# A hybrid decoder layer on one core: the convolutions of token blocks 1 to 3 move into the MLP blocks

## The chip, the cores and the metric

The kernel runs on one core of a Trainium2 chip. The metric is device time in microseconds (us) for one execution of the whole layer; the time before is 3008.22 us, the median of three runs (3004.48 to 3009.67). A core has a matmul engine (PE, with its weight loads shown as PEld), three engines for elementwise work (DVE, ACT, POOL) and SP, whose queue issues the DMAs. Each engine works through its own queue in order.

## The reference

One layer on x of 2048 tokens by 1024 channels, in float32. After an RMSNorm with scale and shift, one projection feeds three mixers, whose outputs are concatenated, projected by W_out and added to x; then a gated MLP and a last RMSNorm. The mixer that matters here is C:

```
a, b = split(u);  h = a * sigmoid(b)                       # 256 channels
h = causal depthwise conv of h over tokens, width 31, + cv_b
h = (h - mean) * rsqrt(var + EPS) * ln_w + ln_b            # over the 256 channels
o_c = h * sigmoid(h)
x = x + g1 * (concat[o_a, o_b, o_c] @ W_out)
h = rmsnorm(x) * (1 + sc2) + sh2
x = x + g2 * (relu(h @ W1)^2 @ W2)
```

Mixer A is a gated linear recurrence (HGRN) with four heads; mixer B is attention over the 256 keys of each query that an indexer scores highest.

## The kernel before

The 2048 tokens are four blocks of 512. First the four input blocks run one after the other, each a series of projection units (24 matmuls of 128x512 for a unit of 128 output channels), whose results are evicted by ACT and DVE. Behind the units run generators in named queues: the HGRN heads ("fast"), the convolution ("conv"), the modulation of later stages ("ada"), and index scores, top-k search and attention of the query tiles ("idx", "tk", "at"). After each unit `step()` gives each queue a credit in ns (`rates`), and a generator runs on until its yields have used the credit up. Then come the out block 0 and four MLP blocks. An MLP block has eight groups g, each with four first-layer units (24 matmuls) and one second-layer part (96 matmuls); towards its end `prep` loads the mixer outputs of the next token block and the out block of that block runs between groups 6 and 7. Index scores, top-k and attention of the later tiles go on behind MLP blocks 0 to 2.

The order in each engine's queue is not the order of the program: a scheduler lays the instructions out by a modelled timeline, with priorities. So any edit moves instructions far from it too.

Projections use each operand as a high and a low part (`hi`, `lo`), three products. Weights are split the first time they are used (ACT casts `whi`, L316; POOL subtracts `wlo`, L317) and the parts are stored in DRAM and reloaded as `wk` later; for the MLP weights the first time is MLP block 0. The hidden tiles are split in the same way (`hh` on ACT, `hl` on POOL, L269).

The convolution of a block (`conv_gen`) has two halves of 128 channels. Of its 31 taps, DVE does the even ones into `cacc` (L552, L564); ACT does the odd ones into `ctap` (L561, or L558 for the first, into `cside`) and POOL adds them into `cside` (L562). There is one `ctap` buffer, so the next tap on ACT waits for POOL's add. Then follow mean and variance by small matmuls, and the LayerNorm and swish, whose result goes to DRAM (`mx_d`) until the out block reads it. The input is the tile `hc` of 30 halo columns and 512 new ones, made by the eviction `ev_ca` (L543); the last 30 columns go to `halo` for the next block. Before, each block's convolution is queued when its `hc` is made, in its own input block, with a rate of 2002 (`CR`), beside the HGRN heads. An HGRN head is a chain between DVE and PE: each of seven levels scales half of q (L638) and half of k (L639) on DVE and then multiplies them on PE (L673, L681).

The tag `xt` of the pool `xio` has four buffers of 128x1024 floats. They hold x of the next input block during an input block, x of the out block, and at the end of an MLP block the final norm's weight, the gate and the rows of the output.

## Time and profile before

| what | us |
|---|---|
| median of three runs | 3008.22 |
| the profiled execution's own time | 3010.64 |
| its span, first to last instruction | 3008.9 |
| PE busy in it | 2828.1 |
| DVE, ACT, POOL busy | 1621.1, 1250.3, 1148.7 |
| mean granted PE clock (1 is full) | 0.971 |

In the profile a row of a table by stage has a stretch of the span, its length, the busy time of each engine in it with the number of instructions, the granted clock of PE and the share of the DMA engines. A row of a group has the line, the engine, the tiles written and read, the shapes and the count, then the busy time and the mean of one in ns, then the idle time of the engine just before them and what ended it. A row of the waits has the waiting engine, tile and line, what released it, and the sum, number and longest of the waits. A row of a timeline has start and length, and in brackets the idle time before it.

In the span the input blocks end at about 1090 us and the out block 0 runs into the first MLP block; MLP blocks 0 to 3 run from about 1140, 1590, 2100 and 2590 us. The taps of the convolutions of blocks 1, 2 and 3 stand between 389 and 483, 671 and 771, and 927 and 1008 us.

### The profile page before, as it was taken

What the parts mean: (1) busy time and instruction counts of PE and PEld (TensorE: products, weight loads), DVE (VectorE), ACT (ScalarE), POOL (GpSimd) and SP (SyncE); (2) the same over time, 40 slices, a digit from 0 to 9 for tenths busy, and PEclk for the clock granted to TensorE, in tenths of its full rate; (3) what the DMA queues carried; (4) which work ended last, traced back from release to release, by engine and by line L of the source; (5) the groups of instructions that cost most, each with busy time, mean ns of one, the idle gap of its engine ahead of it and who ended that gap; (6) DMA issues with size and microseconds to landing.
All of it is one profiled execution on the core that took longest, in us unless ns stands there. A gap on an engine that the chain in (4) does not pass through costs nothing.

```text
span 3008.9 us, 42529 instructions
## 1 busy us (share of the span) xinstructions
PE 2828.1 (94%) x14200; PEld 2343.3 (78%) x14200; DVE 1621.1 (54%) x3306; ACT 1250.3 (42%) x2586; POOL 1148.7 (38%) x1051
## 2 busy tenths in 40 slices
PE   5988989898899989999998999999999999999998
PEld 4867868686787877788776888877788888788887
DVE  7695487868447343847758646485944211221113
ACT  4445545435322325455536443444553333231112
POOL 7574143216313254566547422223432223311112
PEclk9998989999999999999999999999999999999999
DMA  8866666575654586899978966777786667685565
GB/s 284 266 202 208 216 185 204 184 243 180 207 173 152 171 273 213 267 288 291 292 239 278 304 202 205 228 225 229 239 289 209 224 206 229 220 274 178 188 204 187
DMA packets 424199, 681.25 MB, mean 226 GB/s; under 512 B 43351, under 2 KB 171420, under 8 KB 423964
## 3 DMA queue, kind: packets, MB, share of 16 engines
q1 hardware_dynamic: 423808, 678.33, 69.8%
q8 instruction: 113, 1.85, 0.2%
q14 instruction: 122, 1.00, 0.1%
q10 hardware_dynamic: 156, 0.07, 0.0%
HBM read 525.40 MB, written 152.84 MB: 225 GB/s over the span
## 4 chain that ended last, share of the span: by engine, by line
PE 42%; DVE 3%; DMA 2%; issue 1%; ACT 1%; POOL 1%; SPq 0%; POOLq 0%; DVEq 0%; ACTq 0%
PE mm L1252 13%; PE mm L391 13%; PE ax L1252 7%; PE ax L391 4%; PE po L977 1%; PE at L965 1%; PE at L943 1%; PE at L1252 1%; PE ix L786 1%; DVE s L793 1%; DMA xo<-x_d 1%; DMA wk<-wk_d 1%; DMA wraw<-in_mlp_w_dram 0%; SPq L106 0%; DVE acc L1396 0%
## 5 line engine op out<-in xcount | busy, mean ns | idle before, releaser
L391 PE MATMUL mm<-ah,wk 128*128 128x512 f32 x2256 | 602.2, 401 | 15.0 <-DVE adrow L744 4.5
L391 PEld LDWEIGHTS mm<-ah,wk 128*128 128x128 f32 x2256 | 422.7, 191 | 103.0 <-DVE adrow L744 4.7
L317 POOL TENSOR_TENSOR wlo<-wraw,whi 128x512 fp32r<-128x512 f32 x210 | 290.0, 1400 | 170.3 <-ACT whi L316 106.5
L269 POOL TENSOR_TENSOR hl<-hr,hh 128x512 fp32r<-128x512 f32 x128 | 168.7, 1319 | 445.3 <-ACT hh L261 417.2
L975 POOL TENSOR_TENSOR pT<-L,pT 128x512 fp32r<-128x512 f32 (+3 forms) x160 | 197.1, 1234 | 298.0 <-ACT pT L974 186.8
L391 PE MATMUL mm<-al,wk 128*128 128x512 f32 x1128 | 307.9, 396 | 0.0
L793 DVE SCALAR_TENSOR_TENSOR s<-r,iw_s,s 128x512 f32<-128x512 f32 (+3 forms) x266 | 243.8, 916 | 110.7 <-ACT r L788 102.7
L1252 PE MATMUL mm<-wk,hh 128*128 128x512 f32 x920 | 281.0, 399 | 1.7 <-DMA wk<-wk_d 1.3
L391 PEld LDWEIGHTS mm<-al,wk 128*128 128x128 f32 x1128 | 211.5, 191 | 42.8
L945 DVE CUSTOM_DVE_ANT_0 L<-at,bias 128x512 f32<-128x512 f32 (+3 forms) x152 | 93.7, 620 | 223.5 <-PE at L943 179.9
L562 POOL TENSOR_TENSOR cside<-cside,ctap 128x512 f32<-128x512 f32 x112 | 163.1, 1456 | 109.7 <-ACT ctap L561 96.3
L1252 PEld LDWEIGHTS mm<-wk,hh 128*128 128x128 f32 x920 | 170.7, 189 | 41.1 <-DMA wk<-wk_d 2.3
L788 ACT ACTIVATE r<-ix 128x512 f32<-128x512 f32 (+3 forms) x256 | 133.1, 553 | 158.6 <-PE ix L786 120.2
L1396 DVE TENSOR_TENSOR acc<-acc,ax 128x512 f32<-128x512 f32 x81 | 55.4, 683 | 237.2 <-PE ax L1252 236.4
L1376 ACT ACTIVATE hr<-mm 128x512 f32<-128x512 f32 x96 | 57.2, 596 | 301.7 <-PE mm L391 301.0
L316 ACT CAST whi<-wraw 128x512 fp32r<-128x512 f32 x210 | 121.5, 618 | 134.1 <-DMA wraw<-in_mlp_w_dram 40.3
L1252 PE MATMUL ax<-wk,hh 128*128 128x512 f32 x552 | 175.8, 399 | 0.3 <-DVE acc L1396 0.3
L895 DVE TENSOR_SCALAR_CACHE_REDUCE cum<-s,ssm 128x384 bf16<-128x384 f32 (+13 forms) x112 | 165.4, 1477 | 9.4 <-POOL s L797 7.1
L1396 DVE TENSOR_TENSOR acc<-acc,mm 128x512 f32<-128x512 f32 x135 | 91.0, 684 | 143.2 <-PE mm L1252 142.6
L973 ACT COPY L<-at 128x512 f32<-128x512 f32 (+3 forms) x160 | 82.8, 522 | 160.8 <-PE at L965 159.1
L1252 PE MATMUL mm<-wk,hl 128*128 128x512 f32 x460 | 149.1, 397 | 0.0
L959 ACT ACTIVATE L<-L,nmx 128x512 f32<-128x512 f32 (+3 forms) x160 | 103.8, 650 | 107.0 <-DVE nmx L954 106.6
(359 smaller groups left out, 6017.2 us busy)
## 6 DMA issues: line engine op xcount, KB each, us to landing
wk<-wk_d SPq DMA_DIRECT2D x800, 256.0 KB
wk<-wk_d SPq DMA_DIRECT2D x198, 512.0 KB
wk_d<-whi SPq DMA_DIRECT2D x210, 256.0 KB
wk_d<-wlo SPq DMA_DIRECT2D x210, 256.0 KB
wraw<-in_mlp_w_dram SPq DMA_DIRECT2D x68, 512.0 KB
kc<-sk_d SPq DMA_DIRECT2D x112, 256.0 KB
vc<-v_d SPq DMA_DIRECT2D x112, 256.0 KB
adw<-in_ada_w_dram SPq DMA_DIRECT2D x128, 128.0 KB
```

The costliest lines, as they stand in the source:

```text
L269: e.tensor_tensor(lo[:, i:j], src[:, i:j], hi[:, i:j].bitcast(F32), OP.subtract)
L316: A.copy(hi, src)
L317: G.tensor_tensor(lo, src, hi.bitcast(F32), OP.subtract)
L391: T.matmul(ps, ww[k], aa[k], start=(n == 0 and k0 == 0), stop=(n == len(order) - 1 and k1 == NK))
L562: G.tensor_tensor(side, side, tap, OP.add)
L788: A.activation(r[:, :w], ps[:, :w], AF.Relu, scale=32.0 ** -0.5)
L793: V.scalar_tensor_tensor(s[:, c0:c0 + w], r[:, :w], iw, s[:, c0:c0 + w], op0=OP.mult, op1=OP.add)
L895: V.tensor_scalar(dump, s, t, -AIM - i * STEP, op0=OP.is_ge, op1=OP.add, accum_out=d)
L959: A.activation(lt[:, :w], lt[:, :w], AF.Exp, bias=nmx, accum_out=sm[:, cb:cb + 1])
L975: G.tensor_tensor(pT[:, :nt, 1], lv, pT[:, :nt, 0].bitcast(F32), OP.subtract)
L1252: T.matmul(ps, aa[f][:, tok * P:(tok + 1) * P], ww[i], start=(first and n == 0), stop=(last and n == 5))
L1396: V.tensor_tensor(dst, dst, src, OP.add)
```

## The change

`ev_ca` stores `hc` of blocks 1 to 3 in DRAM (`hc_d`), and the generator is queued there for block 0 alone. When MLP block b begins, the generator for block b + 1 is queued, with a rate of 950 (`CM`); what is left of it is run out at `prep`. A convolution there takes four `xt` tiles: two receive `hc` (and hold the small results later), one the two sums of DVE, one the side sum and the tap. Its three small products go to the `at` banks of PSUM. Block 0's convolution stays where it was, with its old tiles. The arithmetic is the same.

```diff
+    hc_d = [[dram([P, TAPS - 1 + TB], F32, f"hc_d{b}_{m}") for m in range(2)] for b in range(NB)]
...
         V.tensor_tensor(hc[:, TAPS - 1:], ps, conv[m], OP.mult)
-        G.tensor_copy(halo[:, m, :], hc[:, TB:])
+        if b + 1 < NB:
+            G.tensor_copy(halo[:, m, :], hc[:, TB:])
+        if b:
+            dma(hc_d[b][m], hc)
         conv[m] = hc
...
+    def conv_tiles_late(b):
+        wide = [xp.tile([P, 2, TB], F32, tag="xt", bufs=4, name=nm("cl")) for _ in range(4)]
+        flat = [w.rearrange("p a n -> p (a n)") for w in wide]
+        hcs = [w[:, :TAPS - 1 + TB] for w in flat[:2]]
+        for m in range(2):
+            dma(hcs[m], hc_d[b][m])
+        work = wide[3]
+        cus = [flat[0][:, :TB], flat[1][:, :TB], work[:, 1], work[:, 0], flat[0][:, :TB], flat[1][:, :TB]]
+        return (hcs, [wide[2][:, m] for m in range(2)], lambda: work[:, 0], lambda: work[:, 1], lambda: cus.pop(0),
+                lambda: flat[0][:, D - 4:], lambda i: ps_at())
...
     def conv_gen(b):
-        accs = []
+        hcs, accs, new_side, new_tap, new_cu, new_rs, ps_c = (conv_tiles_late if b else conv_tiles)(b)
...
-            if ev is ev_ca and m == 1:
+            if ev is ev_ca and m == 1 and b == 0:
                 queues["conv"].append(conv_gen(b))
...
     for b in range(NB):
+        if b + 1 < NB:
+            queues["conv"].append(conv_gen(b + 1))
+            rates["conv"] = CM
         for ev in mlp_block(b):
             if ev == "prep":
+                drain("conv")
                 prep_out(b + 1)
```

The queue of DVE in input block 3, at the levels of HGRN head 0 (`q`, `k`) beside which `hc` is made. Before:

```order
L639 TENSOR_TENSOR k_9583<-k_9583,fb_9806 128x64x4
L564 SCALAR_TENSOR_TENSOR cacc_10417<-hc_9984,cvc,cacc_10417 128x512
L564 SCALAR_TENSOR_TENSOR cacc_9995<-hc_9928,cvc,cacc_9995 128x512
L564 SCALAR_TENSOR_TENSOR cacc_10417<-hc_9984,cvc,cacc_10417 128x512
L564 SCALAR_TENSOR_TENSOR cacc_9995<-hc_9928,cvc,cacc_9995 128x512
L564 SCALAR_TENSOR_TENSOR cacc_10417<-hc_9984,cvc,cacc_10417 128x512
L564 SCALAR_TENSOR_TENSOR cacc_9995<-hc_9928,cvc,cacc_9995 128x512
L612 TENSOR_SCALAR f_10050<-f_10050 128x512
```

And now, at the same two levels and the next one (L659 and L660 are the old L638 and L639, L696 the old L675, L633 the old L612):

```order
L660 TENSOR_TENSOR k_9273<-k_9273,fb_9496 128x64x4
L544 TENSOR_TENSOR hc_9618<-mm_9584,csg_9512 128x512
L696 COPY_PREDICATED at_9466<-lmask,ax_9567 128x32x8
L659 TENSOR_TENSOR q_9310<-q_9310,fb_9496 128x4x8x8
L660 TENSOR_TENSOR k_9273<-k_9273,fb_9496 128x32x8
L544 TENSOR_TENSOR hc_9674<-mm_9640,csg_9565 128x512
L696 COPY_PREDICATED at_9466<-lmask,ax_9597 128x16x16
```

The taps (L564) between one level's k and the next are gone; the levels stand next to each other.

The queue of POOL at the start of MLP block 0, from the first weight half (`wlo`) on. Before:

```order
L317 TENSOR_TENSOR wlo_11905<-wraw_11838,whi_11904 128x512
L317 TENSOR_TENSOR wlo_11909<-wraw_11838,whi_11908 128x512
L317 TENSOR_TENSOR wlo_11962<-wraw_11902,whi_11961 128x512
L269 TENSOR_TENSOR hl_11874<-hr_11875,hh_11873 128x512
L317 TENSOR_TENSOR wlo_11966<-wraw_11902,whi_11965 128x512
L269 TENSOR_TENSOR hl_11938<-hr_11939,hh_11937 128x512
```

Now (L318 and L270 are the old L317 and L269; L584 is the add into the side sum, in an `xt` tile named `cl`):

```order
L584 TENSOR_TENSOR cl_11417<-cl_11417 128x512
L318 TENSOR_TENSOR wlo_11445<-wraw_11367,whi_11444 128x512
L584 TENSOR_TENSOR cl_11417<-cl_11417 128x512 x2
L318 TENSOR_TENSOR wlo_11449<-wraw_11367,whi_11448 128x512
L584 TENSOR_TENSOR cl_11417<-cl_11417 128x512
L318 TENSOR_TENSOR wlo_11506<-wraw_11442,whi_11505 128x512
L270 TENSOR_TENSOR hl_11403<-hr_11404,hh_11402 128x512
L318 TENSOR_TENSOR wlo_11510<-wraw_11442,whi_11509 128x512
L584 TENSOR_TENSOR cl_11417<-cl_11417 128x512
```

The adds of the convolution of block 1 now stand one or two at a time between the weight halves and the hidden tiles of MLP block 0; between the first and the last of its 28 adds stand 30 of the weight halves and 9 of the `hl`. On DVE the taps of that convolution follow each other in the same place:

```order
L586 SCALAR_TENSOR_TENSOR cl_11416<-cl_11414,cvc,cl_11416 128x512
L586 SCALAR_TENSOR_TENSOR cl_11416<-cl_11415,cvc,cl_11416 128x512
L586 SCALAR_TENSOR_TENSOR cl_11416<-cl_11414,cvc,cl_11416 128x512
L586 SCALAR_TENSOR_TENSOR cl_11416<-cl_11415,cvc,cl_11416 128x512
L812 TENSOR_SCALAR s_11429<-r_11434,iw_s 128x512
L586 SCALAR_TENSOR_TENSOR cl_11416<-cl_11414,cvc,cl_11416 128x512
L586 SCALAR_TENSOR_TENSOR cl_11416<-cl_11415,cvc,cl_11416 128x512
```

L586 is the old L564 and L812 the first row of the indexer's scores; of the rows of this convolution on DVE, 25 taps stand in a run ahead of that L812 with one other row among them.

More of the change, by code (lines that the diff above doesn't have):

```diff
@@ L63 @@
 CT = 2
-CR = 2002
+CR, CM = 2002, 950.0
 LP = 0
@@ L543, in ev_ca, with conv_tiles @@
         V.tensor_tensor(hc[:, TAPS - 1:], ps, conv[m], OP.mult)
-        G.tensor_copy(halo[:, m, :], hc[:, TB:])
+        if b + 1 < NB:
+            G.tensor_copy(halo[:, m, :], hc[:, TB:])
+        if b:
+            dma(hc_d[b][m], hc)
         conv[m] = hc
+    def conv_tiles(b):
+        hcs = [conv[m] for m in range(2)]
+        accs = [hp.tile([P, TB], F32, tag=f"csg{m}", bufs=1, name=nm("cacc")) for m in range(2)]
+        return (hcs, accs, lambda: hp.tile([P, TB], F32, tag="cside", bufs=1, name=nm("cside")),
+                lambda: hp.tile([P, TB], F32, tag="ctap", bufs=CB, name=nm("ctap")), lambda: st("cu", 2),
+                lambda: hp.tile([P, 4], F32, tag="crs", bufs=1, name=nm("crs")), ps_xp)
+    def conv_tiles_late(b):
[8 more added lines that the diff above has]
+                lambda: flat[0][:, D - 4:], lambda i: ps_at())
     def conv_gen(b):
-        accs = []
+        hcs, accs, new_side, new_tap, new_cu, new_rs, ps_c = (conv_tiles_late if b else conv_tiles)(b)
         for m in range(2):
-            hc = conv[m]
-            acc = hp.tile([P, TB], F32, tag=f"csg{m}", bufs=1, name=nm("cacc"))
+            hc = hcs[m]
+            acc = accs[m]
             V.tensor_scalar(acc, hc[:, 0:TB], cvc[:, m, 0:1], col("cvb", m), op0=OP.mult, op1=OP.add)
@@ L556, in conv_gen @@
                     if side is None:
-                        side = hp.tile([P, TB], F32, tag="cside", bufs=1, name=nm("cside"))
+                        side = new_side()
                         A.mul(side, hc[:, w:w + TB], cvc[:, m, w:w + 1])
                     else:
-                        tap = hp.tile([P, TB], F32, tag="ctap", bufs=CB, name=nm("ctap"))
+                        tap = new_tap()
                         A.mul(tap, hc[:, w:w + TB], cvc[:, m, w:w + 1])
@@ L569, in conv_gen @@
                 V.tensor_tensor(acc, acc, side, OP.add)
-            accs.append(acc)
         yield 1200
-        tot = st("cside", 1)
+        tot = new_side()
         G.tensor_tensor(tot, accs[0], accs[1], OP.add)
-        pm = ps_xp(4)
+        pm = ps_c(4)
         T.matmul(pm, o256.to_broadcast([P, P]), tot, start=True, stop=True)
@@ L579, in conv_gen @@
         for m in range(2):
-            sq = st("cu", 2)
+            sq = new_cu()
             A.activation(sq, accs[m], AF.Square)
@@ L584, in conv_gen @@
         yield 1500
-        pv = ps_xp(5)
+        pv = ps_c(5)
         for t in range(4):
             T.matmul(pv[:, t:t + 1], sqs[0][:, t * P:(t + 1) * P], ones[:, 0:1], start=True, stop=True)
-        rc = hp.tile([P, 4], F32, tag="crs", bufs=1, name=nm("crs"))
+        rc = new_rs()
         V.tensor_copy(rc, pv[:, :4])
@@ L591, in conv_gen @@
         yield 1500
-        rs = ps_xp(6)
+        rs = ps_c(6)
         for t in range(4):
```

4 lines of the change are left out of this document (2 added, 2 removed).

## The prediction

> **What bounds the kernel now.** I read the page first, then a table of busy time by stage, then the waits of PE and the timelines where PE stands.
>
> ```profile
> span 3008.9 us, 42529 instructions
> PE 2828.1 (94%) x14200; PEld 2343.3 (78%) x14200; DVE 1621.1 (54%) x3306; ACT 1250.3 (42%) x2586; POOL 1148.7 (38%) x1051
> ...
> 300.00:1140.00 840.00, 765.48 (x4447) 653.29 (x4446) 524.11 (x1155) 345.06 (x766) 282.45 (x283) 0.95 0.61 196
> 1140.00:1590.00 450.00, 437.86 (x2002) 355.65 (x2001) 271.16 (x540) 238.86 (x476) 265.61 (x221) 0.99 0.86 273
> 1590.00:2100.00 510.00, 495.75 (x2328) 404.07 (x2327) 322.99 (x654) 237.59 (x501) 178.41 (x167) 0.98 0.74 236
> 2100.00:2590.00 490.00, 483.70 (x2292) 394.64 (x2291) 193.90 (x395) 195.50 (x407) 162.83 (x156) 0.99 0.71 232
> ```
>
> Columns of the stage rows: length, then busy time of PE, PEld, DVE, ACT, POOL, the granted clock, DMA share and GB/s. PE sets the time nearly everywhere. MLP blocks 0, 1 and 2 (the last three rows, each with the out block behind it) leave it idle for 12, 14 and 6 us at a clock of 0.98 to 0.99; the input blocks 1 to 3 (300 to 1140) leave it idle for 75 us of 840 and at 0.95. So there is something to win in the input blocks, and little slack to lose in the MLP blocks. The change takes work of DVE, ACT and POOL from the first place to the second. No matmul of the main stream is added or removed, so only PE's standing and its clock can change.
>
> **Part 1: what leaves the input blocks.** I cut 300 to 1140 at the first and last convolution tap of blocks 1, 2 and 3: the second, fourth and sixth rows hold a convolution each, the others none.
>
> ```profile
> 300.00:389.00 89.00, 88.32 (x531) 76.38 (x530) 42.02 (x120) 46.45 (x108) 17.64 (x35) 0.99 0.69 223
> 389.00:483.00 94.00, 78.83 (x403) 64.63 (x402) 86.70 (x149) 52.90 (x99) 52.13 (x46) 0.89 0.62 190
> 483.00:671.00 188.00, 170.84 (x1064) 148.00 (x1063) 134.60 (x401) 76.89 (x191) 38.00 (x52) 0.96 0.64 205
> 671.00:771.00 100.00, 83.83 (x443) 68.61 (x441) 81.41 (x147) 56.04 (x107) 59.55 (x48) 0.93 0.54 177
> 771.00:927.00 156.00, 148.69 (x906) 129.87 (x907) 58.89 (x137) 41.84 (x109) 25.11 (x25) 0.96 0.59 193
> 927.00:1008.00 81.00, 74.98 (x418) 64.29 (x417) 61.83 (x91) 33.27 (x62) 41.45 (x33) 0.96 0.50 161
> 1008.00:1140.00 132.00, 119.99 (x694) 101.52 (x694) 58.64 (x113) 37.66 (x91) 48.56 (x46) 0.94 0.62 209
> ```
>
> I measure what PE gave as busy time times clock. With a convolution: 78.83 x 0.89 + 83.83 x 0.93 + 74.98 x 0.96 = 220.1 us of full-speed work in 275 us, so 54.9 us lost, 20%. Without: 506.9 in 565, so 58.1 us lost, 10%. DVE is busy for 84% of the first kind of stretch and 52% of the second. What leaves, per group:
>
> ```profile
> L562 POOL TENSOR_TENSOR cside<-cside,ctap 128x512 f32<-128x512 f32 x84 | 122.3, 1455 | 86.6 <-ACT ctap L561 78.0 <-ACT cside L558 6.5 <-DMA mx_d<-r 1.9
> L564 DVE SCALAR_TENSOR_TENSOR cacc<-hc,cvc,cacc 128x512 f32<-128x512 f32 x90 | 91.0, 1032 | 0.3
> L561 ACT ACTIVATE ctap<-hc,cvc 128x512 f32<-128x512 f32 x84 | 60.7, 723 | 78.1 <-POOL cside L562 77.6
> sum 275.00, DVE 99.95 ACT 0.00 POOL 3.62; mean DVE 33.32 ACT 0.00 POOL 1.21
> ```
>
> The last row is the sum over the three stretches for the tile cacc alone: 100 us of DVE, 33.3 a block. POOL loses 122 us of adds and ACT 61 us of taps, besides 78 us in which ACT, which works in order, stood before the next tap because the one ctap buffer was still being read by POOL. Is it these rows that hold PE? Three waits of the stretches 389 to 483 and 671 to 771, and the timeline of the longest wait in the third:
>
> ```profile
> PE ax L695 <- DVE k L639: 4.6, 1, 4.6
> PE mm L391 <- ACT k L611: 3.6, 1, 3.6
> PE mm L391 <- DVE adrow L744: 4.5, 1, 4.5
> ...
> 942.84 1.49 DVE L639 TENSOR_TENSOR k<-k,fb 128x256 f32<-128x256 f32 x1
> 944.25 6.13 DVE L564 SCALAR_TENSOR_TENSOR cacc<-hc,cvc,cacc 128x512 f32<-128x512 f32 x6
> 951.73 2.44 DVE L564 SCALAR_TENSOR_TENSOR cacc<-hc,cvc,cacc 128x512 f32<-128x512 f32 x2
> 954.43 1.84 DVE L564 SCALAR_TENSOR_TENSOR cacc<-hc,cvc,cacc 128x512 f32<-128x512 f32 x1
> 956.86 0.41 DVE L639 TENSOR_TENSOR k<-k,fb 128x256 f32<-128x256 f32 x1
> 957.42 1.94 PE L673 MATMUL ax<-q,k 128*128 128x64 f32 x8 [4.74 <-DVE k L639]
> ```
>
> Between two L639 steps of one HGRN head (14 us apart) DVE did nine taps, 10.4 us, and PE stood 4.74 us for the second step. The four longest waits, 4.7, 4.6, 4.5 and 3.6, are 17.4 us. In the new order of DVE these taps are gone and the HGRN levels follow each other. The value I take: the 220.1 us of full-speed work in the convolution stretches will run at the 90% of the others, in 220.1 / 0.897 = 245.4 us, a gain of **29.6 us**. Ends: 54.9 if nothing at all is lost there any more; 5 if the HGRN chain, which DVE also carries in the stretches without a tap, takes the waits over. The value is nearest to the rows of the same stage without a convolution.
>
> The stretch at 389 has the four longest waits' worst clock, 0.89. The Trainium skill, "TensorE: Matmul & The Clock Gate", section "What's actually happening", has the clock halved only after an idle window of about 3.4 us. By that rule, as an estimate, only those four waits cost clock too, 1.7 us each, and the gain would be 17.4 + 6.8 = 24 us; the rows give more because many short waits go with them.
>
> **Part 2: what arrives in the MLP blocks.** The same 33 us of DVE, 41 us of POOL adds and 20 us of ACT taps stand in MLP blocks 0, 1 and 2, from the first unit of the block. What a loaded DVE costs PE there I read from rows of 60 us:
>
> ```profile
> 1210.00:1270.00 60.00, 56.09 (x240) 44.80 (x239) 50.29 (x118) 30.62 (x56) 31.92 (x26) 0.97 0.79 253
> 1270.00:1330.00 60.00, 59.98 (x278) 49.18 (x277) 31.57 (x75) 35.59 (x68) 40.44 (x35) 1.00 0.96 314
> 1390.00:1450.00 60.00, 60.00 (x286) 49.47 (x285) 46.20 (x94) 36.37 (x76) 40.75 (x36) 1.00 0.94 302
> 1450.00:1510.00 60.00, 57.04 (x261) 46.16 (x260) 47.08 (x94) 30.67 (x61) 33.10 (x28) 1.00 0.88 276
> 1830.00:1890.00 60.00, 60.00 (x283) 49.07 (x282) 48.14 (x106) 25.90 (x55) 14.08 (x15) 1.00 0.69 212
> 2130.00:2190.00 60.00, 55.60 (x257) 43.20 (x257) 49.02 (x89) 32.47 (x66) 27.14 (x21) 0.94 0.68 218
> 2190.00:2250.00 60.00, 59.41 (x291) 48.77 (x290) 26.64 (x50) 32.81 (x72) 21.67 (x21) 1.00 0.85 282
> ```
>
> With DVE at 46 to 50 us (five rows) PE's full-speed work falls short by 5.6, 0, 3.0, 0 and 7.7 us, mean 3.3; with DVE at 27 to 32 (two rows) by 0 and 0.6. So one such window lifted costs 3 us. The new order lays the DVE taps nearly in one run at the start of the block, so I count one window for each block: 3 us for each of the MLP blocks 1 and 2. Spread out at 14 us a window it would be 2.4 windows, 7 us a block.
>
> MLP block 0 is the tight one, because POOL splits the weights there for the first time:
>
> ```profile
> L317 POOL TENSOR_TENSOR wlo<-wraw,whi 128x512 fp32r<-128x512 f32 x210 | 290.0, 1400 | 170.3 <-ACT whi L316 106.5 <-PE mm L1252 20.8 <-PE ax L1252 16.7
> L269 POOL TENSOR_TENSOR hl<-hr,hh 128x512 fp32r<-128x512 f32 x128 | 168.7, 1319 | 445.3 <-ACT hh L261 417.2 <-DMA wk<-wk_d 26.6 <-PE mm L391 1.0
> 2690.46 5.48 PE mm L391 x24
> ...
> 2734.67 5.48 PE mm L391 x24
> ```
>
> In the new order 30 weight halves and 9 hl stand on POOL between the first and the last of the convolution's 28 adds: 30 x 1.400 + 9 x 1.319 + 28 x 1.455 = 94.6 us. PE's work for those 15 weight pieces is 9 first-layer units of 5.45 us and 6 second-layer pieces of (44.2 - 4 x 5.45) / 4 = 5.6 us (the last two rows are one group of eight units apart, 44.2 us), 82.7 us; the stage gives PE 437.9 us for 8 x 44.2 + 45 = 399 us of main stream (the out block's 192 matmuls at the second layer's rate are 45), so 10% other work lies between: 91 us. POOL has no slack there, 94.6 against 91. I take 8 us for this block: 3 as above, and 5, one unit, for weights that come late. Ends: 0, as in the row at 1390 with POOL at 41 of 60; 41 if all adds delay the splits.
>
> The Trainium skill, "SBUF — State Buffer", section "Who interferes with whom", speaks against the move: a DVE instruction with two SBUF inputs waits out a GpSimd instruction that reads SBUF. The trace agrees as far as the taps go (mean 1032 ns where the last one above took 1.84 us). By it, as an estimate, thirty taps beside a POOL that never rests would each last to about 1.8 us, and the run of DVE grow from 33 to some 55 us, 2.2 windows in place of one, 4 us more.
>
> Smaller parts, together 0: six stores and six loads of 128x542 floats (277 KB, at the stages' 196 to 273 GB/s 1.0 to 1.4 us each, 14 us if all lay bare) lie beside DMA engines at 61% and 86%, and a load stands ahead of weights that are asked for a unit early. The x of the out block now waits on SP for the convolution's result to be stored, about half an MLP block before it is used; if that cover were gone, 4 x 524 KB at 236 GB/s, 9 us a block. Three small matmul groups per convolution move with it, and their work is PE's in either place. Where a result of POOL is late for them, PE stands as it does now.
>
> **Sum**, on the profiled execution's own 3010.64 us (span 3008.9): -29.6 + 8 + 3 + 3 = -15.6, so **2995 us**. The median of the runs shown, 3008.22, lies 2.4 us lower; I name **2994**. What a measurement can tell from no change is about 0.2%, 6 us.
>
> **Rivals.** *No change*: the HGRN chain keeps the waits (the stretch 1008 to 1140 loses 9% without a tap), the gain is 10 to 15, the cost 14: 3007 to 3012. For it: half of PE's loss in the input blocks is in stretches without taps. Against: the 10.4 us of taps ahead of that 4.74 us wait. *Deeper*: the stretches lose nothing any more and the MLP rows behave as those at 1390 and 1830: -55 + 5 = -50, 2958. For it: 300 to 389 lost 2%. Against: the other three lost 9 to 15%. *Slower*: POOL becomes the bound of MLP block 0, the splits come late by all 41 us of adds, and the other blocks cost 7 each: -29.6 + 41 + 14 = +25, 3034. For it: 94.6 against 91 us, and DMA at 0.94 to 0.96 in the rows 1270 and 1390, so late weights can't be made up by DMA. Against: POOL stood at 41 of 60 us there with PE at 60.00. It decides from 24 us lost in block 0 on, where 29.6 - 6 is eaten. *The order itself*: every queue after block 0 is laid out anew by the scheduler, worth a few us of either sign; it widens each case.
>
> **How the numbers follow.** Forecast 0.52 (2980 to 3004), no change 0.20, slower 0.15, deeper 0.13. Faster by over 6 us: nearly all of the forecast, all of deeper, a bit of no change, 0.64. Within: most of no change, 0.16. Slower: the slower case and the upper tail of no change, 0.20. Range 2965 to 3022.
>
> **What would show it.** Right: input blocks 1 to 3 shorter by some 30 us, no PE wait of over 4 us there for the HGRN's step on k (L639 now) or for adrow, clock above 0.95 there; MLP block 0 longer by under 10 us. Wrong: the input blocks shorter by under 15 us (the HGRN chain), or PE waits for wlo or wk in MLP block 0 above 20 us in sum (POOL), or waits at the out blocks for x.

## The result, and the profile after

The changed kernel takes **3034.69 us** (median of five runs, 3028.56 to 3041.03), the kernel before 3008.22 (five runs, 3004.48 to 3011.75): ratio 1.0085, 95% interval 1.0068 to 1.0101. It is slower by some 26 us, where 14 us less were forecast. The profiled execution took 3039.32 us.

The page of the kernel after, its span and busy times:

```profile
span 3037.6 us, 42546 instructions
PE 2841.6 (94%) x14200; PEld 2347.8 (77%) x14200; DVE 1598.5 (53%) x3306; ACT 1257.5 (41%) x2594; POOL 1151.5 (38%) x1049
```

The same 14,200 matmuls, DVE and ACT and POOL as busy as before within 23 us. Work has only changed places. Line numbers after are higher, most by 21 or 22: the tap on DVE is L586, the add on POOL L584, the eviction of a hidden unit L1397, the second-layer and out-block matmuls L1273, the step on k L660, the weight half L318.

I divide both executions at the first transposes of each block and take the lengths: input blocks 1 to 3 with out block 0 together are 39.9 us shorter, MLP blocks 0 to 3 are 21.9, 25.1, 18.0 and 3.1 us longer. The gain came, larger than forecast; the price was five times what I had counted. Of the 65 us that MLP blocks 0 to 2 are longer, PE stands idle for some 38, loses some 21 to a lower clock, and works some 7 more.

**Where the gain is.** Waits of PE in the input blocks 1 to 3 after (what waited, on what; sum, number, longest):

```profile
PE ax L694 <- DVE k L660: 11.8, 6, 3.4
```

The 4.7 us wait for the HGRN's step on k and the 4.5 us wait for `adrow` are gone; the longest left for k is 3.4, and no other line of these waits sums to more than 4.6.

**Where the price is, first place.** Stretches in which the DVE taps of the three late convolutions run, after; columns as in the prediction's stage rows (length, PE, PEld, DVE, ACT, POOL busy, clock):

```profile
1105.00:1145.00 40.00, 32.82 (x130) 25.80 (x128) 39.76 (x37) 18.23 (x32) 32.20 (x18) 0.91 0.65 199
1677.00:1721.00 44.00, 37.65 (x175) 30.39 (x174) 43.73 (x62) 23.13 (x47) 25.70 (x21) 0.92 0.69 197
2207.00:2252.00 45.00, 37.87 (x172) 30.05 (x171) 44.80 (x54) 25.03 (x49) 29.09 (x21) 0.92 0.52 176
```

And the kernel before at the same distance from the starts of its blocks:

```profile
1144.00:1184.00 40.00, 39.65 (x176) 32.00 (x177) 11.30 (x13) 23.09 (x50) 23.23 (x19) 1.00 0.96 289
1695.00:1739.00 44.00, 44.00 (x214) 36.26 (x213) 31.06 (x85) 20.08 (x46) 12.00 (x12) 1.00 0.85 265
2199.00:2244.00 45.00, 44.41 (x216) 36.37 (x215) 19.10 (x42) 23.56 (x55) 11.41 (x10) 1.00 0.78 263
```

DVE is busy for 128.3 us of 129. By busy time times clock PE gave 99.3 us of full-speed work in 129, where it gave 128.1 before: 10.1, 9.4 and 10.2 us lost, 29.7 in sum against 0.9. How a DVE that is not on PE's path takes 10 us from it, the timelines of MLP block 0 show, in the order DVE, ACT, PE, POOL (start, length, idle time before it and what ended it):

```profile
1107.61 7.55 DVE L586 SCALAR_TENSOR_TENSOR cl<-cl,cvc,cl 128x512 f32<-128x512 f32 x5
1115.09 0.74 DVE L749 SCALAR_TENSOR_TENSOR r<-ax,cols,gate 128x512 f32<-128x512 f32 x1
1115.75 22.02 DVE L586 SCALAR_TENSOR_TENSOR cl<-cl,cvc,cl 128x512 f32<-128x512 f32 x17
1137.70 0.47 DVE L812 TENSOR_SCALAR s<-r,iw_s 128x512 f32<-128x512 f32 x1
```

```profile
1138.26 0.60 ACT L809 ACTIVATE r<-ix 128x512 f32<-128x512 f32 x1 [6.12 <-DVE s L812]
...
1140.74 0.59 ACT L1397 ACTIVATE hr<-mm 128x512 f32<-128x512 f32 x1
```

```profile
1122.13 1.19 PE L807 MATMUL ix<-ki,qi 96*128 96x512 f32 x2 [3.09 <-DVE cl L586]
...
1138.91 0.79 PE L807 MATMUL ix<-ki,qi 96*128 96x512 f32 x1 [4.09 <-ACT r L809]
...
1147.21 0.50 PE L1273 MATMUL ax<-wlo,hh 128*128 128x512 f32 x1 [2.07 <-POOL wlo L318]
```

```profile
1139.55 6.38 POOL L584 TENSOR_TENSOR cl<-cl 128x512 f32<-128x512 f32 x1 [6.30 <-ACT cl L583]
```

It is a chain of queues. Seventeen taps, 22.0 us, stand on DVE ahead of the first row of the indexer's scores (L812). The scores free the two buffers `r`; without one ACT stands for 6.12 us before L809. Behind that L809 on ACT wait the next tap of the convolution, for which POOL stands 6.30 us, and the eviction of the hidden unit (L1397). PE stands for 4.09 us before an indexer product whose bank ACT has not read, with the main stream behind it in order, and later for the weight half that POOL got to late, behind an add that lasted 6.38 us.

The 3.09 us of the first PE row are put down to a tap, but that product waits for several things at once, and the last of its loads (`qi`, `ki`) landed 0.05 us before that tap ended. The loads had been issued late. SP had stood for the result of L749, which DVE had behind five taps, and issued them behind it:

```profile
SPq L106 <- DVE r L749: 6.6, 1, 6.6
```

```profile
1116.71 1.52 SPq L106 DMA_DIRECT2D qi<-iq_d  x3
```

So the taps held three queues, those of ACT, POOL and SP. No wait here is a wait for the convolution's result.

**Second place: out block 3.** The wait of PE that stands there, and the waits and DMA issues of SP's queue, after:

```profile
PE at L1273 <- DMA wk<-wk_d: 6.0, 1, 6.0
```

```profile
SPq L106 <- DMA mx_d<-ot: 4.0, 1, 4.0
```

```profile
2571.60 4.30 SPq L106 DMA_DIRECT2D wk<-wk_d  x8
2576.00 1.56 SPq L106 DMA_DIRECT2D mx_d<-ot  x2
2577.65 2.20 SPq L106 DMA_DIRECT2D wk<-wk_d  x2
2583.98 0.80 SPq L106 DMA_DIRECT2D mr<-mx_d  x2
```

and the kernel before at that place:

```profile
2541.26 2.95 SPq L106 DMA_DIRECT2D wk<-wk_d  x6
2545.98 0.79 SPq L106 DMA_DIRECT2D mx_d<-ot  x2
2548.16 2.08 SPq L106 DMA_DIRECT2D wk<-wk_d  x4
2551.45 0.79 SPq L106 DMA_DIRECT2D mr<-mx_d  x2
```

The out block starts at 2555.6 after and 2542.9 before. The result of the last query tile's attention is stored (`mx_d<-ot`) 3 us behind that start before, and 20 us behind it after; `mr` is read back from it. In PE's queue the last product of that attention with v, which I call its tail, stood 36 main matmuls ahead of the out block and now stands 42 behind its first one; small transposes into `at` follow it.

The store is not what held the weights: the load that PE needed was issued at 2573.4, in the first of the rows after, ahead of the store, and landed at 2581.1. SP had stood for a product of PE before it could issue that row, and the out block's products into `at` begin late. The wait of SP, and the first of these products after and before:

```profile
SPq L106 <- PE at L1273: 12.9, 5, 11.8
```

```profile
2570.61 0.73 PE L1273 MATMUL at<-wk,mh 128*128 128x512 f32 x2 [0.35 <-ACT ot L1011]
```

```profile
2544.34 0.62 PE L1252 MATMUL at<-wk,mh 128*128 128x512 f32 x2
```

One of the four token tiles of the out block has its sums in an `at` bank, which the attention's transposes also use. Its products began 1.4 us into the out block before and 15.0 us into it after, behind the tail, and SP stood for them until 2571.6. That a weight buffer comes free only with the last of its four tiles fits this; no run tests it by itself. The 4.0 us that SP stood for the store held only `mr`, for which PE stood 1.1 us. A stretch of 60 us around the out block's start, after and then before:

```profile
2540.00:2600.00 60.00, 51.63 (x222) 40.33 (x222) 6.38 (x11) 10.64 (x25) 17.08 (x17) 0.94 0.53 173
```

```profile
2528.00:2588.00 60.00, 60.00 (x264) 48.41 (x263) 8.64 (x13) 6.03 (x12) 16.91 (x18) 1.00 0.68 224
```

11.5 us of full-speed work are lost there, none before. The two places make 40 of the 65 us. About 6 more are the small products of the convolutions, which are PE's own work and moved along: 18 matmuls, some 2 us, for each convolution. The rest lies in short stops. Boundaries between MLP blocks are soft as well: 78 more matmuls run in MLP block 1 than before (2443 for 2365), 18 of them the convolution's and 60 background that the blocks beside it had done, so 25.1 is partly its neighbours'.

### The profile page after: what moved, and what is told of

It reads as the page before. It is cut to its first block, busy times and chain, and to the rows that moved or that the text cites. A ratio compares the mean times of both kernels' runs of the same rounds, so it can differ in the third digit from the quotient of the medians.

```text
span 3037.6 us, 42546 instructions
## 1 busy us (share of the span) xinstructions
PE 2841.6 (94%) x14200; PEld 2347.8 (77%) x14200; DVE 1598.5 (53%) x3306; ACT 1257.5 (41%) x2594; POOL 1151.5 (38%) x1049
## 5 line engine op out<-in xcount | busy, mean ns | idle before, releaser
L318 POOL TENSOR_TENSOR wlo<-wraw,whi 128x512 fp32r<-128x512 f32 x210 | 293.4, 1417 | 137.9 <-ACT whi L317 84.4
L270 POOL TENSOR_TENSOR hl<-hr,hh 128x512 fp32r<-128x512 f32 x128 | 174.8, 1366 | 390.0 <-ACT hh L262 363.3
L1273 PE MATMUL mm<-wk,hh 128*128 128x512 f32 x920 | 285.1, 403 | 3.4 <-ACT acc L1415 2.3
L1273 PEld LDWEIGHTS mm<-wk,hh 128*128 128x128 f32 x920 | 172.5, 191 | 44.0 <-ACT acc L1415 2.7
L809 ACT ACTIVATE r<-ix 128x512 f32<-128x512 f32 (+3 forms) x256 | 134.3, 552 | 162.0 <-PE ix L807 119.2
L317 ACT CAST whi<-wraw 128x512 fp32r<-128x512 f32 x210 | 122.2, 619 | 137.5 <-DMA wraw<-in_mlp_w_dram 44.1
L1273 PE MATMUL ax<-wk,hh 128*128 128x512 f32 x552 | 178.2, 402 | 1.0 <-DMA wk<-wk_d 0.6
L1397 ACT ACTIVATE hr<-mm 128x512 f32<-128x512 f32 x96 | 57.1, 595 | 286.6 <-PE mm L392 282.6
L584 POOL TENSOR_TENSOR cl<-cl 128x512 f32<-128x512 f32 x84 | 126.7, 1508 | 65.3 <-ACT cl L583 54.6
L1273 PE MATMUL mm<-wk,hl 128*128 128x512 f32 x460 | 148.4, 399 | 0.0
```

What stands on the lines that cost most here:

```text
L270: e.tensor_tensor(lo[:, i:j], src[:, i:j], hi[:, i:j].bitcast(F32), OP.subtract)
L317: A.copy(hi, src)
L318: G.tensor_tensor(lo, src, hi.bitcast(F32), OP.subtract)
L584: G.tensor_tensor(side, side, tap, OP.add)
L809: A.activation(r[:, :w], ps[:, :w], AF.Relu, scale=32.0 ** -0.5)
L1273: T.matmul(ps, aa[f][:, tok * P:(tok + 1) * P], ww[i], start=(first and n == 0), stop=(last and n == 5))
```

## The experiments

Every kernel has its runs of the kernel before beside it (medians 3008 to 3011). The stage lengths in this table are those of one profiled execution against the one of before, in us, divided as above. Input block 0, which no edit touches, differs by up to 3 us between them, and the profiled execution lies up to 10 us from its kernel's median (e15: 2994.3 against 3003.9), so a few us in a stage say little.

| run | median | ratio, 95% interval | input 1-3 | MLP 0 | MLP 1 | MLP 2 | MLP 3 |
|---|---|---|---|---|---|---|---|
| after | 3034.7 | 1.0068 to 1.0101 | -39.9 | 21.9 | 25.1 | 18.0 | 3.1 |
| e1_left_out | 2960.8 | 0.9805 to 0.9860 | -45.2 | -9.6 | 4.9 | -1.1 | 0.7 |
| e2_twice | 3089.1 | 1.0226 to 1.0285 | 0.6 | 22.6 | 34.6 | 19.2 | 1.5 |
| e3_block1 | 3018.0 | 1.0004 to 1.0035 | -19.9 | 17.9 | 13.7 | -2.1 | 1.0 |
| e4_block3 | 3037.6 | 1.0048 to 1.0110 | -3.3 | 3.4 | 2.1 | 22.6 | 0.7 |
| e5_paced | 3020.0 | 1.0016 to 1.0040 | -43.9 | 19.0 | 25.0 | 8.0 | 2.1 |
| e6_no_dve | 2996.7 | 0.9950 to 0.9980 | -47.2 | 7.3 | 15.5 | 5.1 | 2.2 |
| e7_no_side | 2995.2 | 0.9935 to 0.9970 | -41.8 | 1.7 | 17.4 | 6.1 | 1.8 |
| e8_b3_ax | 3030.4 | 1.0047 to 1.0086 | -7.5 | 0.9 | -0.6 | 27.8 | 2.1 |
| e9_tail | 3027.6 | 1.0044 to 1.0084 | 0.0 | -1.8 | -1.2 | 14.3 | 6.4 |
| e10_b3_g3 | 3012.4 | 0.9997 to 1.0021 | -4.0 | 0.4 | 0.7 | 6.9 | 1.0 |
| e11_dve_paced | 3021.3 | 1.0024 to 1.0051 | -46.1 | 16.9 | 22.6 | 13.2 | 6.4 |
| e12_dve_run | 3017.8 | 1.0011 to 1.0037 | -45.3 | 15.0 | 22.5 | 13.2 | 3.8 |
| e13_dve_po | 3005.9 | 0.9982 to 1.0012 | -42.3 | 7.7 | 19.9 | 7.3 | 0.6 |
| e14_side_mm | 3008.8 | 0.9977 to 1.0009 | -46.5 | 25.2 | 14.9 | -0.2 | 0.3 |
| e15_dve_mm | 3003.9 | 0.9969 to 0.9993 | -46.6 | 14.3 | 8.6 | 2.1 | 4.6 |
| e16_dve_po9 | 2999.7 | 0.9960 to 0.9982 | -43.7 | 15.2 | 6.3 | 4.2 | 0.3 |
| e17_gap | 2991.3 | 0.9923 to 0.9954 | -41.9 | 4.8 | 13.5 | 1.3 | 2.0 |

### What the two halves of the change are worth

The convolutions of blocks 1 to 3 left out altogether:

```diff
-            dma(hc_d[b][m], hc)
+            dma(mx_d[b][6 + m], hc[:, TAPS - 1:])
...
-        if b + 1 < NB:
+        if False:
             queues["conv"].append(conv_gen(b + 1))
```

> The convolutions of blocks 1 to 3 are left out altogether: their inputs are stored straight into the mixer output, so the kernel does less than the reference. After the change the input blocks ended 40 us earlier and MLP blocks 0, 1 and 2 took 22, 25 and 18 us longer. Theory A (the late convolution's own rows hold PE in the MLP blocks): the 40 us stay, the MLP blocks take what they took before, 2966 to 2972. Theory B (the new layout of all queues, or background work that the shorter input blocks push into the MLP blocks, costs the time): the MLP blocks stay longer by 30 us or more, 2998 to 3010. Theory C (POOL in MLP block 0 alone): as A, 2968.

Measured 2960.8, a little under the range of theory A; with 3034.7 the late convolutions cost 73.9 us. And the opposite, the convolution done in its own input block as before and once more late, with a second result that nothing reads:

```diff
-            if ev is ev_ca and m == 1 and b == 0:
+            if ev is ev_ca and m == 1:
...
-            dma(mx_d[b][6 + m], o)
+            dma((again_d if again else mx_d[b])[6 + m], o)
...
-            queues["conv"].append(conv_gen(b + 1))
+            queues["conv"].append(conv_gen(b + 1, True))
```

> Each convolution of blocks 1 to 3 runs in its input block as before, and a second time in the MLP block as changed, with a result that nothing reads: the price of the late convolution by itself. A: 50 to 65 us above before, 3058 to 3073, spread over MLP blocks 0, 1 and 2. B: within 20 us of before. C: 25 us above, nearly all in MLP block 0.

3089.1, 79 us above the kernel before and above the range of A. So the late convolutions have a price of their own of 74 to 79 us, whatever the input blocks do (their small products, done twice in e2, are part of it), and a new layout of the queues without them (e1) costs nothing. B falls as the account of the whole.

### Which block pays

Only block 1 late (the tests `if b` become `if b in (1,)`), and only block 3:

```diff
-        if b:
+        if b in (1,):
             dma(hc_d[b][m], hc)
...
-        if b + 1 < NB:
+        if b + 1 in (1,):
             queues["conv"].append(conv_gen(b + 1))
```

> Only block 1's convolution is moved, into MLP block 0; blocks 2 and 3 as before. A: the input block gains 12 to 15, MLP block 0 loses 22, so 3013 to 3020. B: the loss appears in MLP blocks 1 and 2 too, 3020 or more. C: the same as A, since POOL is tight only there.

> Only block 3's convolution is moved, into MLP block 2, the block with the least other work on DVE (194 us of 490). A: input block 3 gains 10 to 15, MLP block 2 loses some 18, 3008 to 3016. B: no forecast of its own, a loss also in MLP blocks 0 and 1. C: gains 12 and loses 3, 2996 to 3000.

The time of block 1 alone, 3018.0, lies in A's range, which is C's too, but the sum behind it is another. The input blocks gained 19.9 where 12 to 15 were expected, and MLP block 1, in which no convolution ran late, was 13.7 us longer; 26 of its matmuls (2391 for 2365) are background that MLP block 0 had done before. A loss in a block that has no late work is what B had named, so part of the 25.1 us of MLP block 1 in the changed kernel need not be its own convolution's. Block 3 did not come out as A had it: 3037.6, as slow as all three together, with 22.6 us in MLP block 2, where POOL has no weights to split. C, that POOL in MLP block 0 alone makes the price, falls, and A was short: 15 of these us stand between group 6 and out block 3, the second place of the reading above.

### Taps on which engine

Half of the taps left out, first those of DVE, then those of ACT with POOL's adds:

```diff
-                else:
+                elif b == 0:
                     V.scalar_tensor_tensor(acc, hc[:, w:w + TB], cvc[:, m, w:w + 1], acc,
```

> The changed kernel without the 28 DVE taps of each late convolution after the two first ones (they are left out of the result); the ACT taps and the POOL adds stay. Theory R: the run is gone, 2970 to 2990. Theory S: half of the price goes, 2995 to 3010. Theory Q (the chain of ACT taps and POOL adds is what delays the weights and the evictions): little goes, 3010 to 3030.

```diff
-                    else:
+                    elif b == 0:
                         tap = new_tap()
```

> The changed kernel without the ACT taps and POOL adds of each late convolution but the first of each half (they are left out of the result); the DVE taps stay. Theory R: the run is still there, shorter only by what POOL beside it cost each tap (37 us down to some 25): 2995 to 3020. Theory S: 2995 to 3010. Theory Q: most of the price goes, 2965 to 2985.

2996.7 and 2995.2: the halves take 38 and 39.5 us of the 74 with them. That is theory S in the first run, and in the second the lower edge of R and S; Q falls. The two halves also stretch each other. The tap on DVE, after and without POOL's adds beside it:

```profile
L586 DVE SCALAR_TENSOR_TENSOR cl<-cl,cvc,cl 128x512 f32<-128x512 f32 x90 | 100.6, 1163 | 0.2
```

```profile
L586 DVE SCALAR_TENSOR_TENSOR cl<-cl,cvc,cl 128x512 f32<-128x512 f32 x90 | 81.0, 942 | 0.3
```

POOL's add lasts 1508 ns in the mean after and 1368 ns without the DVE taps.

### The run taken apart

The taps are bound to the hidden units, so that they cannot run ahead; the credit per unit falls from 950 to 700 with it, so two things change:

```diff
+                if b and w % 3 == 1:
+                    cvt = pace["pad"][:, m * 30 + w - 1:m * 30 + w + 2]
+                    V.scalar_tensor_tensor(cvt, pace["r"][:, 0:3], 0.0, cvc[:, m, w:w + 3], op0=OP.mult, op1=OP.add)
...
                 split(r, hi, lo)
+                pace["r"] = r
```

> The changed kernel, with the taps of the late convolutions tied to the hidden units: for every three taps a tiny DVE instruction multiplies three numbers of the newest hidden tile by zero and adds the three tap weights, and the taps read these weights (one more DVE instruction of 128x3 per three taps, 20 a block). The taps can so not run ahead, and stand two or three at a time over five of the eight groups of an MLP block. Theory R (the run of some 25 DVE taps stands in front of the indexer's scores, ACT and PE work in order behind them): most of the late price of 74 us (3034.7 less 2960.8 with the convolutions left out) goes; 2975 to 3000. Theory S (the sum of the late work on ACT, DVE and POOL counts, wherever it stands): the price stays, 3020 to 3045.

3020.0: between the two ranges, 15 us better, 59 us of the price left. R alone is not it. The stretch that lost 10.1 us with the run of taps, in this kernel, and a wait of PE later:

```profile
1105.00:1145.00 40.00, 36.77 (x155) 29.65 (x154) 25.50 (x28) 26.86 (x47) 31.91 (x23) 0.96 0.82 265
```

```profile
PE mm L1282 <- DVE acc L1427: 9.2, 4, 6.5
```

The run's own loss went: PE gives 35.3 us of full-speed work there, not 29.9. But MLP blocks 0 and 1 are as long as with the run (19.0 and 25.0 us more than before, against 21.9 and 25.1). The loss of block 0 now stands around group 3. The longest stop is 6.5 us at 1334 for the add into PE's accumulator (L1427), behind a top-k search that had itself stood for 7.3 us; no tap stands next to it. So the run is where the changed kernel lost 29 us, but these two blocks lose as much without it, and why they do stays open here.

The kernel had a fault of its own, too: in PE's queue its convolution of block 3 ended 27 main matmuls behind the start of out block 3, and MLP block 2 lost 13.5 us there (5.5 ahead at group 6, 8.0 behind at group 7).

### Out block 3 by itself

Three runs on the attention's tail. First the late convolution of block 3 alone with its small products in other banks (`ps_at()` becomes `ps_ax()`), which happens to move the tail back:

> Only the convolution of block 3 is late, as in the run of it alone (3037.6), but its small products go to the ax banks instead of the at banks. Nothing else is edited; the scheduler then lays the last query tile's attention so that its last matmul stands 12 matmuls of the main stream ahead of out block 3, where it stood 42 behind its first one (36 ahead in the kernel before). Theory T (the attention's tail, late in the order of PE, holds out block 3, whose mixer loads wait for its result with weight loads queued behind them on SP): the 15 us that the run lost from group 6 to out block 3 of MLP block 2 fall to 0 to 6, 3022 to 3031. Theory U (the late convolution's own work holds out block 3): 3033 to 3042.

3030.4, within theory T's range for the sum, but not for its reason: out block 3 lost some 9 us instead of 15, and the groups of the same block up to the 5th lost some 19 where they had lost 7. The price moved from one place to the other. Then the kernel before with the attention slowed in MLP block 2:

```diff
+        if b == 2:
+            rates["at"] = 0.7 * R2[2]
         for ev in mlp_block(b):
```

> The kernel before, no convolution moved; only the credit that attention gets after each unit of MLP block 2 is 0.7 of what it was, and its last matmul then stands 72 matmuls of the main stream behind the first of out block 3, not 36 ahead. Theory T: out block 3 loses 10 to 20 us against the kernel before, groups 1 to 6 of MLP block 2 may win some of it, 3012 to 3030. Theory U: nothing of the kind at out block 3, 3004 to 3012.

3027.6, with no convolution moved at all: MLP block 2 is 5.5 us ahead at group 6 and 14.3 behind at group 7. A late tail of the attention is by itself enough to lose that much at out block 3; this part of T is shown. The way that T gives for it is not. PE's longest wait there is 4.6 us for a load of the attention's own (`po` for `vc`), and its wait for `wk` is 0.2 us. The tail is also later than in the changed kernel, 72 main matmuls behind the out block's first one and not 42. Last, block 3 late with both faults mended, from the 24th unit on and spread, with a credit of 1300:

```diff
-            queues["conv"].append(conv_gen(b + 1))
+            later = [24, b + 1]
...
+                if later and later[0] == 0:
+                    queues["conv"].append(conv_gen(later[1]))
+                later = later and [later[0] - 1, later[1]]
                 step()
```

> Only the convolution of block 3 is late; it is queued from the 24th of the 52 units of MLP block 2 before the out block on, where DVE is busy for 11 to 17 us of 60, its taps are tied to the hidden units (tiny DVE instruction per three taps), and its small products go to the ax banks; the attention's last matmul stands 34 matmuls ahead of out block 3. Theory T with theory S (work beside an idle DVE is cheap): MLP block 2 longer by 0 to 6 us, input block 3 shorter by 8 to 11: 2998 to 3008. Theory U: 15 us at out block 3 remain, 3012 to 3020.

3012.4, no measurable difference from before, and by its sum at the edge of theory U. By its stages it is T's: MLP block 2 costs 6.9 us instead of 22.6, and the one wait of PE above 1 us from 2480 us on, around out block 3, is

```profile
PE mm L1282 <- DMA wk<-wk_d: 1.5, 1, 1.5
```

Out block 3 itself loses nothing against the kernel before. The step of 8 us that is left stands ahead of it, between the second-layer parts of groups 5 and 6, and it is work: PE has 256 matmuls there for 222 before, 18 of them the convolution's and 16 the attention's, and is busy for 53.1 us where it was for 46.4. Input block 3 gave 8.5 us, while input blocks 1 and 2, which the edit doesn't touch, were 4.5 us longer in this execution: this move alone has little to win.

### All taps on DVE

The taps of ACT and POOL go to DVE as well: spread (e11, and e13 with the small products in the po bank and a credit of 700), and in a run (e12):

```diff
-                if w % CT == 1:
+                if w % CT == 1 and b not in (1, 2, 3):
```

> All three convolutions late, all 31 taps of each half on DVE (none on ACT and POOL), tied to the hidden units as in the spread run (credit 620 instead of 700 per unit); the attention's last matmul stands 36 matmuls ahead of out block 3, as in the kernel before. Theory P (the pair of POOL adds and DVE taps is what costs: POOL has the weight splits, and taps and adds stretch each other): 2985 to 3002, the floor being 2961 with the convolutions left out plus some 9 us of their small matmuls. Theory S (work of DVE, ACT and POOL counts wherever it stands; 28 more DVE taps of 0.74 a half in place of the adds): 3005 to 3025.

> All three convolutions late as in the changed kernel, not spread, but all 31 taps of each half on DVE: runs of some 60 taps, 44 us, at the start of each MLP block. Theory R (a run in front of the indexer's scores is what costs): 3015 to 3040. Theory P: 2990 to 3008.

> As the spread run with all taps on DVE, with a credit of 700 and the small products in the po bank; the attention's last matmul stands 36 matmuls ahead of out block 3 as well. Theory P: 2985 to 3002, theory S: 3005 to 3025; it tells how far an ordering of the queues that is new but alike moves the time, a few us.

3021.3, 3017.8 and 3005.9. P held in none of the three; e11 and e13 are in the range of S (e13 at its lower edge), e12 in that of R. In e11 and e13 the convolution of block 3 again ended behind the start of out block 3 (36 and 10 main matmuls), worth some 20 and 12 us there. e12 showed something unforeseen: with no add of the convolution on POOL, a weight half came later than ever. DVE, POOL and the wait of PE in MLP block 0:

```profile
1133.59 2.73 DVE L586 SCALAR_TENSOR_TENSOR cl<-cl,cvc,cl 128x512 f32<-128x512 f32 x4
1136.24 0.74 DVE L814 SCALAR_TENSOR_TENSOR s<-r,iw_s,s 128x512 f32<-128x512 f32 x1
```

```profile
1127.66 15.09 POOL L318 TENSOR_TENSOR wlo<-wraw,whi 128x512 fp32r<-128x512 f32 x1 [4.21 <-PE ix L807]
```

```profile
PE ax L1273 <- POOL wlo L318: 10.7, 2, 10.2
```

One subtraction on POOL, 1.4 us elsewhere, lasted 15.09 us while DVE went from one instruction of two SBUF inputs to the next without a pause, and PE stood 10.2 us for it.

### One condition at a time, and the better kernel

Spread, with a credit of 900, and the attention's tail where the kernel before has it. In e14 and e15 the small products go to the mm banks and each convolution ends some 520 main matmuls ahead of its out block; e14 has the taps on DVE and ACT with POOL, e15 all on DVE. e16 is e13 with a credit of 900:

> All three convolutions late, taps on DVE and on ACT with POOL as in the changed kernel, tied to the hidden units, with a credit of 900 per unit and the small products in the mm banks. In the order of PE each convolution ends 520 main matmuls ahead of its out block and the attention's last matmul stands 36 ahead of out block 3. Theory T (attention's tail and the convolution's own lateness made the loss at out block 3) with S (the rest of the price stays): 3006 to 3018, with no jump at out block 3. Theory P (POOL adds beside the weight splits, and taps stretching each other, cost most): as much or more, 3012 to 3025.

> As the run before it in everything but this: all taps on DVE, none on ACT and POOL. Theory P: 10 to 25 us less than that run, 2988 to 3002. Theory S: equal to it within 6 us.

> As the spread run with all taps on DVE and the po bank (3005.9), with a credit of 900 instead of 700 per unit, so that the convolution of block 3 ends 210 main matmuls ahead of out block 3 and not behind its start. Theory T: the 12 us that it lost at out block 3 fall to 0 to 4, 2993 to 3002. If something else loses them: 3003 to 3010.

3008.8: spreading, the early end, the other banks and the tail together bring the changed kernel from 3034.7 to the time before, with the taps where they were; MLP block 2 costs nothing any more (18.0 to -0.2), MLP block 0 as much as ever (25.2). All on DVE, 3003.9: 4.9 us less, with intervals that overlap, so the engine of the taps is worth little (S), not the 10 to 25 of P. e16 with 2999.7 is under both kernels; its loss at out block 3 is 0.9 us where e13 had 12.1, as T had it.

What stayed in MLP block 0 was a step of some 10 us between the second-layer parts of groups 1 and 3. The wait of PE in e16 and what DVE did then:

```profile
PE ax L1282 <- DVE acc L1427: 12.1, 2, 6.1
```

```profile
1189.78 1.27 DVE L925 TENSOR_SCALAR_CACHE_REDUCE cum<-s,ssm 128x1024 bf16<-128x1024 f32 x1
...
1190.98 0.75 DVE L823 SCALAR_TENSOR_TENSOR s<-r,iw_s,s 128x512 f32<-128x512 f32 x1
1192.31 0.75 DVE L595 SCALAR_TENSOR_TENSOR cl<-cl,cl,cl 128x512 f32<-128x512 f32 x1
1192.97 0.68 DVE L1427 TENSOR_TENSOR acc<-acc,ax 128x512 f32<-128x512 f32 x1
```

Top-k search (L925), indexer scores (L823) and taps (L595) follow each other without a gap, ahead of the add that frees PE's accumulator (L1427). With the convolutions left out (e1) DVE's load in three stretches of MLP block 0 is:

```profile
1080.00:1160.00 80.00, 75.17 (x355) 61.17 (x355) 34.75 (x48) 42.02 (x83) 42.36 (x35) 0.92 0.75 238
1160.00:1240.00 80.00, 77.45 (x335) 62.11 (x334) 65.08 (x164) 40.77 (x75) 45.06 (x35) 0.98 0.88 277
1240.00:1400.00 160.00, 159.44 (x748) 130.67 (x748) 93.57 (x180) 96.33 (x194) 109.03 (x92) 1.00 0.96 292
```

The middle one has 15 us free of 80. So the taps are kept out of it:

```diff
+                n_step += 1
+                if b == 0:
+                    rates["conv"] = 1300.0 if n_step <= 12 else 0.0 if n_step <= 26 else 900.0
                 step()
```

> As the best spread run (2999.7; all taps on DVE, po bank, credit 900), except that in MLP block 0 the convolution gets a credit of 1300 in the first 12 units, none in the next 14, and 900 from there on. With the convolutions left out DVE is busy for 35 of 80 us in the first of these stretches of MLP block 0, for 35 of 40 and 30 of 40 in the second, 93 of 160 in the third. Theory F (the price of block 0 stands where DVE is full): the step of 12 us at groups 3 and 4 of that block goes, 2987 to 2996. If the taps cost the same wherever they stand: 2997 to 3003.

**2991.3 us** (six runs, 2988.33 to 2995.87), ratio 0.9938, 0.9923 to 0.9954: faster than the kernel before by 0.6%, the forecast's figure by another road. The wait for the add fell to:

```profile
PE ax L1282 <- DVE acc L1427: 3.7, 1, 3.7
```

MLP block 0 costs 4.8 instead of 15.2; MLP block 1 13.5 instead of 6.3, with 30 matmuls more in it and 30 fewer in block 0, so part of both differences is background that slid across the boundary. Against e16 the step near group 3 is gone, and the intervals of the two ratios do not touch. F is borne out by the time, the step and this wait. The profiled executions of the two, 2993.99 and 2992.75, happen to lie 1.2 us apart, so the table cannot show where the 8 us between the medians went.

## Why the prediction was wrong

**Part 1 (-29.6 us) was right, and low.** The input blocks gave 39.9 us, of which some 6 are the small products, which come back in the MLP blocks. PE gives 92% of full-speed work between 300 and 1081 after, where I had taken 90% for the stretches of the taps. The signs named for this part came: no wait over 4 us for k or `adrow`, a clock of 0.97. The reason given, taps between the HGRN's levels, is borne out in part: PE's waits for the step on k fell from 22.8 to 12.9 us, and the rest of the gain I have not traced to rows. The estimate of 24 us by the Trainium skill, "TensorE: Matmul & The Clock Gate", section "What's actually happening", was further off than the rows' 29.6.

**Part 2 (+14) failed, at this step: "one such window lifted costs 3 us", and one window for each block.** The late convolutions cost 74 us (e1) where 14 were counted. The 3 us came from rows in which DVE was busy for 46 to 50 of 60 us with its work mixed. A run is another thing: 40 us of 40. It lost 10.1, 9.4 and 10.2 us. A row of the kernel before with a DVE as full as that stood in the same table of 60 us rows:

```profile
1590.00:1650.00 60.00, 50.08 (x224) 39.45 (x223) 56.58 (x106) 36.73 (x69) 43.27 (x37) 0.89 0.81 265
```

With DVE at 56.58 of 60 us PE falls short by 15.4 us. The start of MLP block 1 stands in it too, so not all of that is DVE's, but it is five times the value that I took; nor were the rows of 46 to 50 five, since that of 2070 to 2130, 46.20 on DVE, is 3.8 us short. The sign named for MLP block 0, longer by under 10 us, failed with 21.9.

The working asked how much of DVE the taps take, not what stands behind them in DVE's queue. I had the answer before me: the quoted order showed 25 taps ahead of the indexer's L812, and the prediction did not ask who waits for that row. It was ACT, then POOL and PE, and through their queues the main stream. That is how the run cost 29 us in this kernel. It is not the whole of the price, for e5 has no run and its MLP blocks 0 and 1 are as long; taking out either half of the taps takes out half of the price (e6, e7), so what was mis-sized is the late work as such.

**The 5 us for late weights** were about right in size: PE waited 3.5 us for `wlo` in MLP block 0. But 2.07 of them stand behind the add of 6.38 us, at the end of the chain of queues, and not behind a POOL with too much work.

**The smaller parts at 0** missed out block 3. There was no wait for x, the sign that I named, but the scheduler's new order put the attention's tail 78 main matmuls later, and 11.5 us were lost around it. I had granted "the order itself" a few us. e9 shows that such a shift alone can cost 14 in that block.

**The rivals.** *Slower* named the time, 3034, by luck, since its place was wrong: it had POOL as the bound of MLP block 0 with 41 us, and 7 for each other block. e4 loses 22.6 in block 2, where no weights are split, and e12, with no such adds on POOL, loses 15.0 in block 0. *Slower* had the gain too small by 10 us and block 0 too dear by 19, which made up for blocks 1 and 2. *Deeper* was right that the input blocks give more than my value, but its -55 is further from the measured -39.9 than my -29.6. In the sum, 3008.22 less 15.6 is 2992.6, not the 2994 that I named; that changes nothing here.

**The estimate by the Trainium skill**, "SBUF — State Buffer", section "Who interferes with whom", was right in direction: the taps stretch beside POOL (1163 against 942 ns, and 1.30 us in the run of seventeen). In size the run of taps in block 0 became 37 us, not 55. PE lost 10 us there through what stood behind it, more than the 3 us of its window and the 4 that this estimate added.

What stays open: with the two places and the small products 46 of the 65 us have a home; the rest lies in short stops that I have not separated, it is not known why MLP blocks 0 and 1 are as long without the run (e5), and the split of what is left in e17 (2991 against 2961 without the convolutions) between blocks 0 and 1 is blurred by the background that slides between them.

## What to carry to other kernels

Work that is moved beside an engine with free time must be priced by what stands behind it in that engine's queue, and by who waits for that: here 37 us of taps with nobody waiting for their result cost PE 10 us, through three queues. Breaking up the run alone did not bring that back. A scheduler that sees no waiter runs such work ahead in one block; tying it to data that come late spreads it. Spread, with all taps on one engine, an early end and kept out of a stretch in which that engine is already full, the move goes from 0.9% slower to 0.6% faster. After any such move, look at the last piece of every background job before each place that reads its result: it is late by what the scheduler pushed back.

## What the runs showed of the hardware

A POOL subtraction of 128x512 that takes 1.4 us lasted 15.09 us while DVE went through a row of instructions with two SBUF inputs (e12), and PE's own wait of 10.2 us for it bears out its length. The trace doesn't name what held it. In the changed kernel an add of POOL lasted 6.38 us beside such a row, but beside the seventeen taps the adds of POOL took some 1.7 us and the taps 1.30, so it does not always come to this. The Trainium skill, "SBUF — State Buffer", section "🎯 Summary: rules for kernel authors", has the second of two such instructions to issue wait until the first finishes; if that is the cause, POOL was passed over by the whole row.

Two stops of PE after, each with the stretch behind it (length, PE busy, and the clock behind the five busy times):

```profile
1098.40:1101.20 2.80, 0.16 (x2) 0.14 (x2) 1.87 (x3) 1.84 (x5) 1.97 (x4) 1.00 0.00 0
1101.20:1104.70 3.50, 3.50 (x13) 3.01 (x13) 2.01 (x3) 2.47 (x6) 1.96 (x2) 0.52 0.55 163
...
1119.00:1121.70 2.70, 0.04 (x1) 0.00 (x0) 2.70 (x2) 0.00 (x0) 2.70 (x3) 1.00 0.81 200
1121.80:1125.20 3.40, 3.07 (x7) 2.48 (x8) 3.40 (x3) 1.15 (x3) 3.39 (x3) 0.50 1.09 345
```

These stops, 2.6 and 3.1 us between two matmuls, were each followed by 3.4 us at half clock, 1.7 us of work more than their own length. Not every stop is: one of 2.30 us at 1711.5 in the same execution and one of 2.96 us at 1467.3 in the kernel before were followed by none, while one of 2.26 us at 687.3 in the kernel before was. What decides is not shown. The idle window of about 3.4 us that the Trainium skill gives for it ("TensorE: Matmul & The Clock Gate", section "What's actually happening") is longer than these stops, and with it I had left them out of the estimate of 24 us.
